# A hybrid recurrent/FFN trunk on one core: the order of loads at the front, one ring for late weights, and turned outputs inside y

## The chip, the core and the metric

The kernel runs on one core of a Trainium2 chip, in one launch. The time is the device time of one execution in microseconds, as the median of repeated runs. One execution more was taken with a profile; it has a time of its own, and all durations of single instructions come from it.

## What is computed

The reference is two residual layers over 2048 latent tokens of width 1024 with a prefix of 256 context tokens. Layer 0 is a bidirectional gated linear recurrence (HGRN2, 8 heads of 128, chunks of 64) and a gated FFN with convolution; layer 1, another mixer, is absent here (DEPTH is 1). Cut to what matters:

```python
D_MODEL, SEQ, CTX_LEN, HEADS, D_FF, CHUNK = 1024, 2048, 256, 8, 2816, 64
# adaLN: shift, scale and gate rows come from SiLU(c) @ w_ada (context: SiLU(c_ctx))
h = modulate(rmsnorm(x, g), shift, scale)          # latent and context
q, zf_fwd, zf_bwd, v, g = split(h @ w_in, 5)       # q = silu(q)
f = lb + (1 - lb) * sigmoid(zf);  k = 1 - f        # per direction
# S_t = diag(f_t) S_{t-1} + k_t v_t^T,  o_t = S_t^T q_t, both directions,
# each direction starting from its final context state
o = o_fwd + o_bwd
y = (rmsnorm(o per head) * silu(g)) @ w_out
x = x + gate1 * y
x = x + gate2 * convffn(modulate(rmsnorm(x), shift2, scale2))
```

The output is the latent stream, 2048 x 1024, in float32.

## The kernel before

Tokens are worked in 16 tiles of 128 (index t; the context is t = -2, -1). Every product is made of three matmuls: `split` (L76) writes an operand as a rounded high part, by ScalarE (L77), and the rest, by VectorE (L78); high x high, high x low and low x high are summed in PSUM. So each weight and each activation passes ScalarE and then VectorE before TensorE (PE) can use it. Five engines run their own instructions in order; the order on each engine is fixed at compile time, after the program's order and priorities. DMAs are issued by SP (queue rows named SPq) or by ScalarE (ACTq), also in order: an instruction that waits holds back what stands behind it on its engine.

Front (L179 to L230). The first two of six rows of the modulation are `sil` times w_ada. 16 loads of 512 KB go into tiles `wada`, in turn by ScalarE and SP, interleaved with 64 matmuls (L202) into four PSUM rows `mps`; the sigmoid that makes `sil` stands ahead of the loads on ScalarE's queue. Three early token tiles are loaded between them (`early_x`: load, square with a sum at L97, root on VectorE and GpSimd at L73 and L74, scale at L100). Four copies `m` (L209), 16 transposes `mt` (L212) and small sums give scale A1 and shift B1 (L215 to L217). With these, `transpose_mod` (L104) turns a token tile into `hm` (PE at L109, ScalarE at L113 or VectorE at L116), and `put_tok` (L147) splits `hm` into the tokens `tok`. Tiles 1 to 4 are squared and scaled ahead of their turn.

`put_tok` keeps tiles 0 to 7 in SBUF. Tiles 8 to 15 go through one staging tile, tag `stg` (one buffer), whose content SP stores to DRAM. `normalize` needs a tile to hold the squares, which nobody reads (`junk`): for `load_x` it comes from the same tag `stg`.

Scan (`mixer_scan`, L264, to about 1283 us). Two halves g of the tokens, and in each 8 heads. For each head five weight blocks are loaded (`load_w`, L166: `raw` of pool `rawp` with two buffers, SP at L168) and split; `acc` (L322) runs 8 x 3 matmuls per block of 512 tokens (L327 to L329), and after each k a `tick` runs what an agenda holds for that time. The results feed ScalarE copies (vt L465, kt L459, v L472, q and g L367), VectorE scans (S L380) and small matmuls (tr L471 and L457, kv L530, o L555). Heads 2 to 5 of the first half make the tokens 8 to 15 (`make_tok`, L338) in pairs.

In the second half `ada_rest` (L582) makes the other four modulation rows. Here 32 loads of w_ada go by SP (L589) through `raw`, and VectorE accumulates (L591, L593); each row is then stored. `out_weight` (L613) prepares the output projection's weight: parts 0 to 3 through `raw`, parts 4 to 7 in `wraw`, a tile that takes the context tokens' place (tag `cxt`) when they are no longer needed; these four are split behind the scan. `keep_gate` (L572) stores each head's gates to DRAM, by SP (L577).

Output stage (`mixer_out`, about 1283 to 1560 us). The tiles go from 15 down to 0. For each, `load_stash` (L876) brings `kq` and `og` from DRAM into two buffers each. `heads` (L881) multiplies by the backward state (oi, L895), adds into og (L899), squares (L902), updates the state (L904), sums (L907) and scales og by the root (VectorE L912, ScalarE L914). `heads_T` (L917) turns og (tp, L924), multiplies by the gate (L926) and splits into `ghl`. `residual(n)` (L930) is y: 24 matmuls for each of two halves n (L935 to L937), added to the latent (L938). The loop turns tile t-1 at the start of the iteration of t, ahead of `heads(t-2)`. norm2 and the stores of the FFN's operands lie beside it. The FFN follows and runs to the end.

Of the kernel before, what the change touches and what calls it, by code (L numbers as in the profile page):

```python
# [11 lines left out]
F32 = mybir.dt.float32  # L12
# [33 lines left out]
def body(ctx, tc, a, out):  # L46
# [125 lines left out]

    def load_x(xt, t):
        x_tile(xt, t)
        junk = xp.tile([128, D], F32, name="junk", tag="stg", bufs=1)
        normalize(xt, junk, gp, on_act=True)
# [4 lines left out]
    with ExitStack() as c0:  # L181
        p0s = pool_(c0, "p0s", space=PSUM)
        act.activation(sil, vec[:, V_C:V_C + 16], AF.Sigmoid)
        dve.tensor_tensor(sil, sil, vec[:, V_C:V_C + 16], OP.mult)
        silv = sil.rearrange("p (two k) -> p k two", two=2)
# [3 lines left out]
        def early_x(t):  # L189
# [3 lines left out]
            load_x(staged[t], t)  # L193

        for k in range(KT):
            for i in range(2):
                n = 2 * k + i
                wt = ada[n // 4][:, n % 4]
                (sp if i else act).dma_start(
                    wt, a["w_ada"][k * 128:(k + 1) * 128, i * D:(i + 1) * D])  # L200
                for n in range(2):
                    pe.matmul(mps[2 * i + n], silv[:, k, :], wt[:, n * 512:(n + 1) * 512],  # L202
                              start=k == 0, stop=k == KT - 1)
            if 3 <= k < 6:
                early_x(k - 5)
        head0 = {ty: load_w(0, ty) for ty in HEAD0[:2]}
# [7 lines left out]
        for i in (1, 0):  # L214
            dve.tensor_tensor(B1[i], mt[:, 0:8, i], vec[:, V_BA:V_BA + 8], OP.add)  # L215
            dve.tensor_tensor(A1[i], mt[:, 8:16, i], vec[:, V_BA + 8:V_BA + 16], OP.add)
            dve.scalar_tensor_tensor(A1[i], A1[i], 1.0, vec[:, V_NG:V_NG + 8], OP.add, OP.mult)  # L217
        hms = [xp.tile([128, KT, 128], F32, name="hm", tag="hm", bufs=1),
               xp.tile([128, KT, 128], F32, name="hm", tag="xt", bufs=1),
# [7 lines left out]
        with tc.issue_after(ada_done.ins):  # L227
            head0.update({ty: load_w(0, ty) for ty in HEAD0[2:]})
        for t in range(1, 5):
            early_x(t)  # L230

# [32 lines left out]
    def mixer_scan():  # L264
# [73 lines left out]
        def make_tok(t, xt=None):  # L338

            got = [xt]  # L340
            hms = []

            def load():
                got[0] = xp.tile([128, D], F32, name="xt", tag="xt", bufs=1)
                load_x(got[0], t)

            def put(g):
                if g == 0:
                    hms.append(xp.tile([128, KT, 128], F32, name="hm", tag="hm", bufs=1))
                transpose_mod(got[0], hms[0], g, ps, A1[0], B1[0], "tr", 1, g)  # L350
                put_tok(hms[0], t, g)

            puts = [lambda: put(0), lambda: put(1)]
            return puts if xt is not None else [load] + puts
# [217 lines left out]
        def keep_gate(h, t0, g):  # L572
            for i in range(UT):
                if is_late(h, t0 + i):
                    pool.tensor_copy(late[:, 1], g[:, i])
                else:
                    sp.dma_start(stash[t0 + i][:, 1, h, 1], g[:, i])  # L577

# [3 lines left out]
        def ada_rest():  # L582

            for i in range(4):
                acc_ = xp.tile([128, D], F32, name="acc", tag="xt", bufs=1)
                c = (2 + i) * D
                for k in range(KT):
                    raw = rawp.tile([128, D], F32, name="raw", tag="raw")
                    sp.dma_start(raw, a["w_ada"][k * 128:(k + 1) * 128, c:c + D])  # L589
                    if k == 0:  # L590
                        dve.tensor_scalar(acc_, raw, sil[:, k:k + 1], None, OP.mult)  # L591
                    else:
                        dve.scalar_tensor_tensor(acc_, raw, sil[:, k:k + 1], acc_, OP.mult, OP.add)  # L593
                    if k < KT - 1:
                        yield
                row = rawp.tile([1, D], F32, name="row", tag="raw")
                for n in range(2):
# [12 lines left out]

        wraw = []

        def out_weight(k):  # L613

            if k < 4:
                raw = rawp.tile([128, D], F32, name="raw", tag="raw")
            else:
                if not wraw:
                    wraw.append(hq.tile([128, 4, D], F32, name="wraw", tag="cxt", bufs=1))
                raw = wraw[0][:, k - 4]  # L620
            sp.dma_start(raw, a["w_out"][k * 128:(k + 1) * 128, :])
# [100 lines left out]
        for k in range(4, KT):  # L722
            split(w_out_part("h", k), w_out_part("l", k), wraw[0][:, k - 4])

# [139 lines left out]
    def mixer_out(c3):  # L864
# [64 lines left out]

        def residual(n, lat, gh, gl):  # L930

            cs = slice(n * 512, (n + 1) * 512)
            y = ps.tile([128, 512], F32, name="y", tag="y")
            for k in range(KT):
                pe.matmul(y, gh[:, k], w_out_part("h", k)[:, cs], start=k == 0, stop=False)  # L935
                pe.matmul(y, gh[:, k], w_out_part("l", k)[:, cs], start=False, stop=False)
                pe.matmul(y, gl[:, k], w_out_part("h", k)[:, cs], start=False, stop=k == KT - 1)  # L937
            dve.tensor_tensor(lat[:, cs], lat[:, cs], y, OP.add)  # L938

# [62 lines left out]
        def load_lat(t):  # L1002
            lat = wn.tile([128, D], F32, name="lat", tag="lat")
            sp.dma_start(lat, a["x"][t * 128:(t + 1) * 128])
            return lat

        next_lat = load_lat(NT - 1)
        for t in range(NT - 1, -1, -1):
            lat = next_lat
            steps = ()  # L1010
            if prev is not None:
                xn = wn.tile([128, D], F32, name="xn", tag="xn", bufs=1)
                steps = norm_steps(prev, xn)
            if t and t < NT - 1:
                gs.append(heads_T(t - 1, ogs.pop(0)))
            if t > 1:
# [6 lines left out]
            g = gs.pop(0)  # L1023
            residual(0, lat, *g)
            if t == NT - 1:
                gs.append(heads_T(t - 1, ogs.pop(0)))
            if t > 2:
# [519 lines left out]
```

## Time and profile before

| | us |
|---|---|
| median of 3 runs | 2827.68 |
| lowest, highest | 2827.45, 2831.03 |
| profiled execution, its own time | 2832.5 |
| its span | 2830.8 |
| mean granted TensorE clock | 0.986 |

Times in a profile are microseconds from the start of the span, and the profiled execution has 1.7 us around it. A row of the timeline gives start, duration, engine, line, operation, output and input with their shape, a count, and in brackets how long the engine had been idle and who released it. A row of waits gives the engine and its line, what it waited for, the total, how often, and the longest. PE is TensorE, PEld its weight load, DVE VectorE, ACT ScalarE, POOL GpSimd, SP SyncE.

### The profile page before, as it was taken

The page shows a single profiled execution, that of the slowest core. Times are in us where ns is not written, and L with a number is a line of the kernel's source. Part 1 is how long each engine was busy: PE and PEld are TensorE (multiplying, and loading weights), DVE is VectorE, ACT ScalarE, POOL GpSimd, SP SyncE. Part 2 cuts the span into 40 slices and gives each one's busy share as a digit, 9 for nine tenths or more (in the row PEclk, how much of TensorE's full clock was granted, in tenths as well). Part 3 has the DMA queues.
Part 4 walks back from the last instruction along what each step waited for, and adds up shares of the span by engine and source line. Part 5 has one row for each costly group of instructions (what it writes and reads, how often), then busy time and mean ns, then how long its engine had stood idle before and what let it go on. Part 6 is the DMA issues. An engine that isn't in the chain of part 4 may idle for free.

```text
span 2830.8 us, 41935 instructions
## 1 busy us (share of the span) xinstructions
PE 2742.5 (97%) x16072; PEld 2274.9 (80%) x16072; DVE 1981.7 (70%) x2804; ACT 1151.0 (41%) x1910; POOL 560.1 (20%) x882
## 2 busy tenths in 40 slices
PE   7999999999999999998999899999999999999998
PEld 3788888888888788886888688888888888877887
DVE  3655556656666667657887788877877777576887
ACT  5424343433232223334656444444444444333343
POOL 2111101111111111111110443333344331000001
PEclk8999999999999999998999999999999999999999
DMA  5122232213533424216777422226322223987663
GB/s 224 49 69 88 87 112 90 89 59 126 202 89 94 129 81 127 90 54 237 278 294 293 186 90 90 84 69 231 141 86 90 90 86 105 321 286 251 194 200 123
DMA packets 223777, 402.18 MB, mean 142 GB/s; under 512 B 29012, under 2 KB 136404, under 8 KB 217816
## 3 DMA queue, kind: packets, MB, share of 16 engines
q1 hardware_dynamic: 220552, 391.24, 41.5%
q10 hardware_dynamic: 3024, 8.26, 0.8%
q8 instruction: 126, 2.06, 0.3%
q14 instruction: 75, 0.61, 0.1%
HBM read 289.04 MB, written 110.38 MB: 141 GB/s over the span
## 4 chain that ended last, share of the span: by engine, by line
PE 74%; DMA 11%; DVE 9%; issue 2%; ACT 2%; POOL 1%; SPq 1%; DVEq 0%; POOLq 0%; ACTq 0%
PE z L327 9%; PE z L329 9%; PE z L328 9%; PE zd L777 3%; PE zd L779 3%; PE zd L780 3%; PE zc L777 3%; PE zc L780 3%; PE zc L779 3%; PE za L777 3%; PE za L780 3%; PE za L779 3%; DMA lr<-m 2%; PE kv L530 2%; PE y L1377 2%
## 5 line engine op out<-in xcount | busy, mean ns | idle before, releaser
L327 PE MATMUL z<-tok,w 128*128 128x512 f32 x1280 | 517.6, 405 | 0.0
L329 PE MATMUL z<-tok,w 128*128 128x512 f32 x1280 | 503.7, 394 | 0.5 <-DVE w L78 0.5
L328 PE MATMUL z<-tok,w 128*128 128x512 f32 x1280 | 503.6, 393 | 0.0
L78 DVE TENSOR_TENSOR w<-raw,w 128x512 fp32r<-128x512 f32 (+1 forms) x260 | 239.5, 925 | 142.1 <-ACT w L77 139.8
L329 PEld LDWEIGHTS z<-tok,w 128*128 128x128 f32 x1280 | 242.0, 189 | 52.3 <-DVE w L78 1.0
L327 PEld LDWEIGHTS z<-tok,w 128*128 128x128 f32 x1280 | 242.8, 190 | 48.4 <-issue 3.6
L328 PEld LDWEIGHTS z<-tok,w 128*128 128x128 f32 x1280 | 242.7, 190 | 44.8 <-issue 0.2
L77 ACT ACTIVATE w<-raw 128x512 fp32r<-128x512 f32 (+1 forms) x260 | 195.9, 760 | 186.6 <-PE zd L780 77.3
L1377 PE MATMUL y<-wd,mh 128*128 128x512 f32 x600 | 234.4, 391 | 3.6 <-ACT X L1412 3.3
L1379 PE MATMUL y<-wd,ml 128*128 128x512 f32 x600 | 234.5, 391 | 1.2 <-DVE ml L78 1.2
L1378 PE MATMUL y<-wd,mh 128*128 128x512 f32 x600 | 234.0, 390 | 0.0
L78 DVE TENSOR_TENSOR w<-s,w 128x512 fp32r<-128x512 f32 x126 | 121.4, 968 | 53.8 <-ACT w L77 53.0
L380 DVE TENSOR_TENSOR_SCAN S<-F,d 128x528 f32<-128x528 f32 (+1 forms) x80 | 91.6, 1145 | 91.2 <-ACT F L363 90.6
L777 PE MATMUL zc<-rT,w 128*128 128x512 f32 x352 | 137.1, 389 | 1.2 <-DVE uv L1264 1.0
L779 PE MATMUL zc<-rT,w 128*128 128x512 f32 x352 | 136.9, 389 | 0.0
L780 PE MATMUL zc<-rT,w 128*128 128x512 f32 x352 | 136.9, 389 | 0.0
L1377 PEld LDWEIGHTS y<-wd,mh 128*128 128x128 f32 x600 | 113.0, 188 | 28.1 <-ACT X L1412 4.1
L77 ACT ACTIVATE w<-s 128x512 fp32r<-128x512 f32 x126 | 78.2, 627 | 138.5 <-POOL s L833 81.9
L1379 PEld LDWEIGHTS y<-wd,ml 128*128 128x128 f32 x600 | 112.9, 188 | 26.5 <-DVE ml L78 3.0
L1378 PEld LDWEIGHTS y<-wd,mh 128*128 128x128 f32 x600 | 113.0, 188 | 23.5
L777 PE MATMUL za<-rB,w 128*128 128x512 f32 x336 | 130.7, 389 | 0.0
L779 PE MATMUL za<-rB,w 128*128 128x512 f32 x336 | 130.7, 389 | 0.0
(323 smaller groups left out, 6223.3 us busy)
## 6 DMA issues: line engine op xcount, KB each, us to landing
raw<-in_w_up_dram SPq DMA_DIRECT2D x88, 512.0 KB, 3.9
raw<-in_w_in_dram SPq DMA_DIRECT2D x80, 512.0 KB, 3.9
lr<-m SPq DMA_DIRECT2D x49, 512.0 KB, 5.7
m<-r SPq DMA_DIRECT2D x66, 256.0 KB, 4.4
raw<-in_w_ada_dram SPq DMA_DIRECT2D x32, 512.0 KB, 3.9
kq<-stash SPq DMA_DIRECT2D x15, 1024.0 KB, 6.4
og<-stash SPq DMA_DIRECT2D x15, 1024.0 KB, 5.4
u<-in_w_down_dram SPq DMA_DIRECT2D x51, 256.0 KB, 3.8
```

The source lines that it names most:

```text
L77: act.activation(h, src, AF.Copy)
L78: dve.tensor_tensor(l, src, h.bitcast(F32), OP.subtract)
L327: pe.matmul(z, w[:, 0, k], h, start=k == 0, stop=False, skip_group_check=True)
L328: pe.matmul(z, w[:, 0, k], l, start=False, stop=False, skip_group_check=True)
L329: pe.matmul(z, w[:, 1, k], h, start=False, stop=k == KT - 1, skip_group_check=True)
L380: dve.tensor_tensor_scan(flat(S[:, d]), flat(F[:, d]), flat(d1[:, 0:ns]), 0.0, OP.mult, OP.max)
L777: pe.matmul(o, w[:, 0, k], r[:, :, 0, k], start=start and k == 0, stop=False, skip_group_check=True)
L779: pe.matmul(o, w[:, 0, k], r[:, :, 1, k], start=False, stop=False, skip_group_check=True)
L780: pe.matmul(o, w[:, 1, k], r[:, :, 0, k], start=False, stop=k == 3, skip_group_check=True)
L1377: pe.matmul(z, lh, rh, start=start, stop=False, skip_group_check=True)
L1378: pe.matmul(z, lh, rl, start=False, stop=False, skip_group_check=True)
L1379: pe.matmul(z, ll, rh, start=False, stop=stop, skip_group_check=True)
```

## The change

Front: all 16 loads of w_ada are issued first, eight by ScalarE and eight by SP, and the sigmoid comes behind them; the three early tiles follow. Squares of tiles 1 to 4 are issued behind the four copies `m`. Squares: a tile made by `make_tok` puts its squares into the `hm` tile that it will fill anyway, no longer into `stg`. Ring: w_ada's later rows, the stored rows and parts 4 to 7 of the output weight take turns in a ring of four tiles in the context's place; `raw` keeps w_in and the parts 0 to 3. Gates: the last head's gates of tiles 8 to 15 are stored by ScalarE. Output stage: `heads_T(t-1)` is called in the middle of the first half of y, after 12 of its 24 matmuls, instead of at the start of the iteration.

```diff
--- before.py
+++ after.py
@@ -170,9 +170,13 @@
         split(w[:, 0], w[:, 1], raw.rearrange("p (k n) -> p k n", k=KT))
         return w
 
-    def load_x(xt, t):
+    def new_hm():
+        return xp.tile([128, KT, 128], F32, name="hm", tag="hm", bufs=1)
+
+    def load_x(xt, t, hm=None):
         x_tile(xt, t)
-        junk = xp.tile([128, D], F32, name="junk", tag="stg", bufs=1)
+        junk = hm.rearrange("p k n -> p (k n)") if hm is not None else \
+            xp.tile([128, D], F32, name="junk", tag="stg", bufs=1)
         normalize(xt, junk, gp, on_act=True)
 
 
@@ -180,8 +184,6 @@
     staged = {}
     with ExitStack() as c0:
         p0s = pool_(c0, "p0s", space=PSUM)
-        act.activation(sil, vec[:, V_C:V_C + 16], AF.Sigmoid)
-        dve.tensor_tensor(sil, sil, vec[:, V_C:V_C + 16], OP.mult)
         silv = sil.rearrange("p (two k) -> p k two", two=2)
         mps = [p0s.tile([2, 512], F32, name=f"mps{n}") for n in range(4)]
         ada = [place(i, [128, 4, D], F32, "wada") for i in range(4)]
@@ -192,17 +194,20 @@
             staged[t] = gp.tile([128, D], F32, name="x0", tag=tag, bufs=1 if tag == "kd" else 2)
             load_x(staged[t], t)
 
+        wts = [ada[n // 4][:, n % 4] for n in range(2 * KT)]
+        for n, wt in enumerate(wts):
+            (sp if n % 2 else act).dma_start(
+                wt, a["w_ada"][n // 2 * 128:(n // 2 + 1) * 128, n % 2 * D:(n % 2 + 1) * D])
+        act.activation(sil, vec[:, V_C:V_C + 16], AF.Sigmoid)
+        dve.tensor_tensor(sil, sil, vec[:, V_C:V_C + 16], OP.mult)
+        for t in range(-2, 1):
+            early_x(t)
         for k in range(KT):
             for i in range(2):
-                n = 2 * k + i
-                wt = ada[n // 4][:, n % 4]
-                (sp if i else act).dma_start(
-                    wt, a["w_ada"][k * 128:(k + 1) * 128, i * D:(i + 1) * D])
                 for n in range(2):
-                    pe.matmul(mps[2 * i + n], silv[:, k, :], wt[:, n * 512:(n + 1) * 512],
+                    pe.matmul(mps[2 * i + n], silv[:, k, :],
+                              wts[2 * k + i][:, n * 512:(n + 1) * 512],
                               start=k == 0, stop=k == KT - 1)
-            if 3 <= k < 6:
-                early_x(k - 5)
         head0 = {ty: load_w(0, ty) for ty in HEAD0[:2]}
         m2 = [gp.tile([2, 512], F32, name="m2", tag="qg"[n // 2], bufs=2) for n in range(4)]
         for n in range(4):
@@ -215,7 +220,7 @@
             dve.tensor_tensor(B1[i], mt[:, 0:8, i], vec[:, V_BA:V_BA + 8], OP.add)
             dve.tensor_tensor(A1[i], mt[:, 8:16, i], vec[:, V_BA + 8:V_BA + 16], OP.add)
             dve.scalar_tensor_tensor(A1[i], A1[i], 1.0, vec[:, V_NG:V_NG + 8], OP.add, OP.mult)
-        hms = [xp.tile([128, KT, 128], F32, name="hm", tag="hm", bufs=1),
+        hms = [new_hm(),
                xp.tile([128, KT, 128], F32, name="hm", tag="xt", bufs=1),
                gp.tile([128, KT, 128], F32, name="hm", tag="S", bufs=1)]
         for g in range(2):
@@ -226,8 +231,8 @@
                 put_tok(hm, t, g)
         with tc.issue_after(ada_done.ins):
             head0.update({ty: load_w(0, ty) for ty in HEAD0[2:]})
-        for t in range(1, 5):
-            early_x(t)
+            for t in range(1, 5):
+                early_x(t)
 
 
         l0, l1 = vec[:, V_LB:V_LB + 16], vec[:, V_LB + 16:V_LB + 32]
@@ -342,11 +347,12 @@
 
             def load():
                 got[0] = xp.tile([128, D], F32, name="xt", tag="xt", bufs=1)
-                load_x(got[0], t)
+                hms.append(new_hm())
+                load_x(got[0], t, hms[0])
 
             def put(g):
-                if g == 0:
-                    hms.append(xp.tile([128, KT, 128], F32, name="hm", tag="hm", bufs=1))
+                if not hms:
+                    hms.append(new_hm())
                 transpose_mod(got[0], hms[0], g, ps, A1[0], B1[0], "tr", 1, g)
                 put_tok(hms[0], t, g)
 
@@ -574,7 +580,16 @@
                 if is_late(h, t0 + i):
                     pool.tensor_copy(late[:, 1], g[:, i])
                 else:
-                    sp.dma_start(stash[t0 + i][:, 1, h, 1], g[:, i])
+                    (act if h == NH - 1 and t0 >= HT else sp).dma_start(
+                        stash[t0 + i][:, 1, h, 1], g[:, i])
+
+        spare = []
+
+        def spare_raw():
+            if not spare:
+                spare.extend([hq.tile([128, 4, D], F32, name="spare", tag="cxt", bufs=1), 0])
+            spare[1] += 1
+            return spare[0][:, (spare[1] - 1) % 4]
 
         ones = small("ones", (128, 1))
         pool.memset(ones, 1.0)
@@ -585,7 +600,7 @@
                 acc_ = xp.tile([128, D], F32, name="acc", tag="xt", bufs=1)
                 c = (2 + i) * D
                 for k in range(KT):
-                    raw = rawp.tile([128, D], F32, name="raw", tag="raw")
+                    raw = spare_raw()
                     sp.dma_start(raw, a["w_ada"][k * 128:(k + 1) * 128, c:c + D])
                     if k == 0:
                         dve.tensor_scalar(acc_, raw, sil[:, k:k + 1], None, OP.mult)
@@ -593,7 +608,7 @@
                         dve.scalar_tensor_tensor(acc_, raw, sil[:, k:k + 1], acc_, OP.mult, OP.add)
                     if k < KT - 1:
                         yield
-                row = rawp.tile([1, D], F32, name="row", tag="raw")
+                row = spare_raw()[0:1]
                 for n in range(2):
                     z = ps.tile([1, 512], F32, name="z", tag="pj", bufs=3)
                     pe.matmul(z, ones, acc_[:, n * 512:(n + 1) * 512], start=True, stop=True)
@@ -608,16 +623,14 @@
             gate_row(g1, 0, 2 * D)
             g1s.append(g1)
 
-        wraw = []
+        wraw = {}
 
         def out_weight(k):
 
             if k < 4:
                 raw = rawp.tile([128, D], F32, name="raw", tag="raw")
             else:
-                if not wraw:
-                    wraw.append(hq.tile([128, 4, D], F32, name="wraw", tag="cxt", bufs=1))
-                raw = wraw[0][:, k - 4]
+                raw = wraw[k] = spare_raw()
             sp.dma_start(raw, a["w_out"][k * 128:(k + 1) * 128, :])
             dve.scalar_tensor_tensor(raw, raw, vec[:, V_GN:V_GN + 1], g1s[0], OP.mult, OP.mult)
             if k < 4:
@@ -720,7 +733,7 @@
                 head(g, h)
         run(1 << 30)
         for k in range(4, KT):
-            split(w_out_part("h", k), w_out_part("l", k), wraw[0][:, k - 4])
+            split(w_out_part("h", k), w_out_part("l", k), wraw[k])
 
     mixer_scan()
     c1.close()
@@ -927,7 +940,7 @@
                 split(gh[:, hs], gl[:, hs], g)
             return gh, gl
 
-        def residual(n, lat, gh, gl):
+        def residual(n, lat, gh, gl, between=None):
 
             cs = slice(n * 512, (n + 1) * 512)
             y = ps.tile([128, 512], F32, name="y", tag="y")
@@ -935,6 +948,8 @@
                 pe.matmul(y, gh[:, k], w_out_part("h", k)[:, cs], start=k == 0, stop=False)
                 pe.matmul(y, gh[:, k], w_out_part("l", k)[:, cs], start=False, stop=False)
                 pe.matmul(y, gl[:, k], w_out_part("h", k)[:, cs], start=False, stop=k == KT - 1)
+                if k == KT // 2 - 1 and between:
+                    between()
             dve.tensor_tensor(lat[:, cs], lat[:, cs], y, OP.add)
 
         def norm_steps(lat, xn):
@@ -1004,6 +1019,9 @@
             sp.dma_start(lat, a["x"][t * 128:(t + 1) * 128])
             return lat
 
+        def turn():
+            gs.append(heads_T(t - 1, ogs.pop(0)))
+
         next_lat = load_lat(NT - 1)
         for t in range(NT - 1, -1, -1):
             lat = next_lat
@@ -1011,8 +1029,6 @@
             if prev is not None:
                 xn = wn.tile([128, D], F32, name="xn", tag="xn", bufs=1)
                 steps = norm_steps(prev, xn)
-            if t and t < NT - 1:
-                gs.append(heads_T(t - 1, ogs.pop(0)))
             if t > 1:
                 ogs.append(heads(t - 2, steps))
             else:
@@ -1021,9 +1037,9 @@
             if t:
                 next_lat = load_lat(t - 1)
             g = gs.pop(0)
-            residual(0, lat, *g)
+            residual(0, lat, *g, between=turn if 0 < t < NT - 1 else None)
             if t == NT - 1:
-                gs.append(heads_T(t - 1, ogs.pop(0)))
+                turn()
             if t > 2:
                 gts[t - 3] = load_stash(1, t - 3)
             if t == 1:
```

## The prediction

> **What bounds the kernel now.** I read the page first: how full TensorE is.
>
> ```profile
> span 2830.8 us, 41935 instructions
> PE 2742.5 (97%) x16072; PEld 2274.9 (80%) x16072; DVE 1981.7 (70%) x2804; ACT 1151.0 (41%) x1910; POOL 560.1 (20%) x882
> ```
>
> TensorE stands idle for 2830.8 - 2742.5 = 88.3 us of the span. The change removes no matmul, so it can win only from these 88.3 us and from time at a reduced clock. The waits of PE, grouped, say which stalls they are (engine and line, releaser: total us, times, longest).
>
> ```profile
> PE tr L471 <- ACT vt L465: 13.0, 5, 3.1
> PE mt L212 <- ACT m L209: 9.5, 1, 9.5
> PE oi L895 <- DMA kq<-stash: 9.3, 1, 9.3
> PE tp L924 <- ACT og L914: 6.0, 5, 1.3
> PE tp L924 <- DVE og L912: 1.6, 2, 1.2
> PE tp L924 <- PE y L937: 0.9, 1, 0.9
> ```
>
> These are 40.3 of the 88.3 us, and each belongs to one part of the change: values waiting for their copy in the scan (13.0), modulation rows at the front (9.5), the first load of the output stage (9.3), and the turning of the gated outputs (6.0 + 1.6 + 0.9 = 8.5). So I cost the change stall by stall. A cost counts only where it reaches PE.
>
> **A. Front.** The rows are the timeline's (start, duration, engine, line), then the loads' own row (duration of an issue: least, median, most) and two windows (PE, PEld, DVE, ACT and POOL busy; granted clock, DMA share, GB/s).
>
> ```profile
> 1.73 1.28 ACT L183 ACT_TABLE_LOAD   x1 [1.73 <-PEq L1538]
> 4.40 5.12 ACTq L199 DMA_DIRECT2D wada<-in_w_ada_dram  x4
> 5.00 28.92 PE L202 MATMUL mps<-wada,sil 128*2 128x512 f32 x64 [5.00 <-DVE sil L184]
> 39.55 1.06 ACT L97 ACTIVATE junk<-x 128x1024 f32<-128x1024 f32 x1 [1.48 <-DMA x<-in_x_dram]
> 44.66 1.05 ACT L209 ACTIVATE m<-mps 2x512 f32<-2x512 f32 x2
> 47.52 0.17 DVE L215 TENSOR_TENSOR B<-mt,vec 128x8 f32<-128x8 f32 x1 [2.51 <-PE mt L212]
> L199 ACTq DMA_DIRECT2D wada<-in_w_ada_dram x8: 334/353/460, 0.8 to 20.2; - x8
> 8.00:12.00 4.00, 4.00 (x11) 0.85 (x10) 1.07 (x4) 0.00 (x0) 4.00 (x8) 1.00 1.02 419
> 40.00:44.00 4.00, 0.62 (x6) 0.65 (x7) 0.15 (x1) 3.08 (x6) 0.55 (x1) 0.50 0.01 2
> ```
>
> Before, PE multiplies from 5.00 to 33.92; then the copies of the four m rows stand in ACT's order behind squares such as that at 39.55, and the shift B is ready at 47.52. After, the copies come before those squares. But now the sigmoid, on which every mps matmul waits, stands behind eight load issues on ACT. Issues are not free: the four from 4.40 held the queue 5.12 us where one takes 0.35, so a later issue waits for an earlier load to land. By the compiled program the last of ACT's eight waits for the seventh load of all. A 512 KB load takes 0.524 MB / 419 GB/s = 1.25 us; if the first lands just before 5.0, the seventh lands near 5.0 + 6 x 1.25 = 12.5. With the issue (0.35), the table load (1.28) and sigmoid and product (0.4), PE starts near 14.6 and ends at 14.6 + 28.9 = 43.5, 9.6 us later than before. The 9.5 us wait falls to about 1; four copies at 0.53 and the turning then bring B at about 46 instead of 47.5. PE no longer idles into the 0.50 clock of the second window, worth some 1 to 2 us more. Against that, the squares and scalings of four tiles (about 2.4 us each, 9.6 us of ACT) now stand behind 46, in front of the tokens that they feed. I take -1, with -4 (all of the 1.5 and the clock) and +5 (half of the squares on the path) as ends. Moving SP's loads ahead of its x loads costs nothing more: DMA stands at 1.02 of its engines, and the order alone changes.
>
> **B. The square's junk tile.** The rows: ACT's timeline, PE's windows behind the stall, ACT's waits, and ACT at the other tile of a pair.
>
> ```profile
> 291.24 1.06 ACT L97 ACTIVATE junk<-xt 128x1024 f32<-128x1024 f32 x1 [6.28 <-DMA tok<-stg]
> 294.00:296.00 2.00, 2.00 (x7) 1.53 (x6) 0.00 (x0) 0.86 (x2) 0.00 (x0) 0.59 0.00 0
> 296.00:298.00 2.00, 2.00 (x11) 1.89 (x10) 0.00 (x0) 0.00 (x0) 0.00 (x0) 0.56 0.00 0
> ACT junk L97 <- DMA tok<-stg: 18.7, 3, 6.3
> 250.59 0.60 ACT L459 ACTIVATE kt<-tr 128x512 f32<-128x512 f32 x1 [1.09 <-PE tr L457]
> ```
>
> Three times ACT stands about 6.2 us (18.7 in all) because the square writes its unused output into the tile that still waits for the store of tokens; the copy of vt (L465) is behind it. These are three of the five vt waits: 13.0 less the two of the later stage (4.9, below) gives 8.1 us. Each is followed by 4 us at a clock of 0.59 and 0.56, which loses 4 x (1 - 0.575) = 1.7 us. Junk in the hm tile needs no store to finish, only the split of the tile before, so all three go: 8.1 + 3 x 1.7 = 13.2 us at most. The Trainium skill (TensorE: Matmul & The Clock Gate, Part 1) says that the clock halves after an idle window of about 3.4 us; by that these gaps of 2.7 us would cost no clock and B would be worth 8.1 alone. The two windows say otherwise, and the trace decides. Cost: at the other tile of four pairs the square, now early, stands ahead of the copy at 250.59 and can hold it by part of a square, 0.7 us each, up to 2.8. I take -13.2 + 2.2 = -11, with -13 and -6 as ends (clock loss not regained).
>
> **C. Rows of w_ada, 720 to 1190 us.** ACT's waits, one of them in its place, and PE's waits from 700 to 1000.
>
> ```profile
> ACT w L77 <- DMA raw<-in_w_in_dram: 53.9, 19, 7.2
> 979.49 1.06 ACT L77 ACTIVATE w<-raw 128x1024 fp32r<-128x1024 f32 x1 [7.21 <-DMA raw<-in_w_in_dram]
> PE tr L471 <- ACT vt L465: 4.9, 2, 3.1
> PE tr L457 <- ACT kt L459: 1.6, 1, 1.6
> PE kv L530 <- ACT v L472: 1.3, 1, 1.3
> PE o L555 <- DVE states L533: 1.0, 1, 1.0
> PE z L329 <- DVE w L78: 0.5, 1, 0.5
> ```
>
> Before, w_in loads (next head) alternate with w_ada loads in two raw buffers, so a weight is late by up to 7.21 us, and ACT, in order, holds vt, kt and v behind it. PE loses 4.9 + 1.6 + 1.3 + 1.0 + 0.5 = 9.3 us, and about 1.5 of clock by the price in B for its one long gap. With the ring in the context's place w_in keeps both raw buffers, as in the half before 720, where no PE wait on a weight's load shows. But the compiled order now bunches w_ada: runs of four to ten loads on SP, each waiting for DVE to free a slot, with stores and w_in loads behind them, and up to three accumulations in a row on DVE ahead of a scan. Three are about 3 x 1.28 = 3.8 us, where before they stood singly. I take -6: the 10.8, less one new stall of the size of 979.49's (3.1 and 1.6 of clock, together 4.7). Ends: -11 and +8 (four such stalls).
>
> **D. Turning inside y.** PE and ACT at one tile, SP's reload of og, its use by DVE, the two ends of one y matmul, and the load's landing (page, last column).
>
> ```profile
> 1396.22 1.06 PE L924 MATMUL tp<-ident,og 128*128 128x128 f32 x8 [1.27 <-ACT og L914]
> 1395.43 1.28 ACT L914 ACTIVATE og<-og,rs 128x128 f32<-128x128 f32 x4 [5.87 <-POOL rs L74]
> 1418.69 0.32 SPq L876 DMA_DIRECT2D og<-stash  x1
> 1428.44 1.48 DVE L899 TENSOR_TENSOR og<-og,oi 128x512 f32<-128x512 f32 x2
> 1385.30 0.39 PE L937 MATMUL y<-wo,ghl 128*128 128x512 f32 x1
> 1385.53 0.39 PE L935 MATMUL y<-wo,ghl 128*128 128x512 f32 x1
> og<-stash SPq DMA_DIRECT2D x15, 1024.0 KB, 5.4
> ```
>
> PE reaches tp about 1.3 us before L914 gives its first output, tile after tile. Turned after 12 matmuls of y it comes 12 x 0.23 = 2.8 us later, behind oi too, so the wait of 1.3 is covered with over a microsecond to spare: up to -8.5 us for the loop. The cost lies on SP: og's buffer comes free that much later, some 4.5 us with oi. In the shorter case above og is issued at 1418.69, lands at 1424.1 and is read at 1428.44: 4.3 us to spare, all but used up. What then is late is L899, whose chain to L914 has itself gained about 3 us, so little should reach PE. I take -6, ends -8.5 and +3.
>
> **E, F. The stage's two ends.** First load and first use; then the first w_up weight.
>
> ```profile
> 1287.12 0.38 SPq L876 DMA_DIRECT2D kq<-stash  x1
> 1290.61 0.32 SPq L876 DMA_DIRECT2D og<-stash  x1
> 1295.53 0.69 DVE L899 TENSOR_TENSOR og<-og,oi 128x512 f32<-128x512 f32 x1 [0.43 <-DMA og<-stash]
> 1536.92 0.63 ACT L77 ACTIVATE w<-raw 128x512 fp32r<-128x512 f32 x1 [1.65 <-DMA raw<-in_w_up_dram]
> ```
>
> With the last gates stored by ACT, SP is spared their issues and reaches kq about 2 us earlier (five at 0.4). But the first y hangs on og, issued at 1290.61 behind DVE's last splits of the output weight, and those splits are behind ACT's copies, now behind seven store issues at some 0.4 us. E: -1, ends -4 and +3. The Trainium skill (DMA: Bandwidth & Descriptors, Issuing engines are not separate DMA queues) says that another issuing engine saves only the time of the issue; that is E's whole gain here. F: the first w_up loads take og's place, released about 3 us later, and ACT waits 1.65 on one already: +1, ends -1 and +4. What follows (the FFN) has the same program.
>
> **The sum.** -1 - 11 - 6 - 6 - 1 + 1 = -24 us. The profiled execution took 2832.5 us (2830.8 and 1.7 around it) and becomes 2808.5; it was 4.8 us above the median of the timed runs, 2827.7, which becomes 2803.7. I forecast 2804 us.
>
> **Rivals.** *Half the gain.* The copies and junk do what they should, but C gives nothing (bunches replace the late weights) and the front pays its late squares: -24 + 6 + 6 = -12, some 2816. For it: PE starts its first matmul 9.6 us later, and C's SP runs. Chance 0.23. *More gain*: every part near its good end except the front, -4 - 13 - 10 - 8 - 2 = -37, 2791; for it, no engine but PE is over 70% busy; against, each gain uncovers the next wait. Chance 0.1. *Slower, by the bunches.* SP is in order: if each run of w_ada loads blocks it until DVE has freed slots, the w_in loads behind it are late at every run, and PE stalls as at 979.49, 4.7 us a time. There are some nine runs. The other five parts give -18, so the sign turns when C reaches +18, or (18 + 10.8) / 4.7, six stalls; with all nine, C is 42 - 10.8 = +31 and the time 2827.7 + 13 = 2841. Against it: DVE is 70% busy, and in the compiled order the accumulations of a run stand ahead of the next weights' splits. Chance 0.1. *Not what it says*: the parts move stalls without removing them, B included (hm is still being split when the square comes): within 5 us of 2827.7. Against: hm's split ends long before 291. Chance 0.05.
>
> **How the numbers follow.** The forecast has 0.52, with 2804 and its own 2797 to 2811. The range 2790 to 2821 takes in half the gain and most of the larger one, and leaves out the slower rival, the idle one and small tails, under 2 in 10. About 0.2% (5.7 us) can be told from no change. Faster: 0.52 + 0.23 + 0.1 = 0.85; same 0.05; slower 0.10.
>
> **What would show it.** Right: no vt wait near 291, 375 and 459 and no low clock behind; B1 at about 46 with mps from 14 to 44; no wait of ACT on w_in loads above 3 us after 720; no tp wait on og. Wrong: PE waits on w or F near SP's w_ada runs, oi waiting for kq or og in the output stage, the first tokens well after 75.

## The result and the profile after

| | before | after |
|---|---|---|
| median of 12 runs, us | 2826.24 | 2836.40 |
| lowest to highest | 2820.88 to 2831.03 | 2830.76 to 2841.79 |
| profiled execution, span | 2832.5, 2830.8 | 2833.5, 2831.8 |
| ratio, 95% interval | | 1.0038, 1.0029 to 1.0048 |

The change makes the kernel slower by 10 us; 24 less were forecast. The two profiled executions differ by 1.0 us only: that of before is longer than any of its 12 timed runs, 6.3 above their median, and that of after is 2.9 below its own. So the traces are compared by stages, and the times by the ratios.

The page of the kernel after, its first lines:

```profile
span 2831.8 us, 41982 instructions
PE 2735.7 (97%) x16072; PEld 2267.8 (80%) x16072; DVE 1978.9 (70%) x2804; ACT 1149.9 (41%) x1910; POOL 563.6 (20%) x882
```

PE is idle for 96.1 us as against 88.3. The waits of PE after:

```profile
PE mps L208 <- DVE sil L202: 15.2, 1, 15.2
PE y L948 <- DVE lat L953: 13.4, 7, 4.6
PE oi L908 <- DMA kq<-stash: 9.8, 1, 9.8
PE tp L109 <- DVE xn L962: 8.5, 7, 2.1
PE tp L109 <- ACT xt L100: 5.8, 3, 2.3
```

The vt waits (13.0), the mt wait (9.5) and the tp waits on og (8.5) are gone. In their place PE waits for the sigmoid, for scaled tiles (xt), and in the output stage for the latent and the norm. Where time was lost and won follows from the starts of like matmuls, counted one by one over PE's timeline from 0 (us, after less before; +2.2 at z 80 means that this z matmul starts 2.2 us later in the changed kernel):

| matmul | after - before | the stretch up to it | us |
|---|---|---|---|
| z 80 | +2.2 | front, tiles 1 to 4 | +2.2 |
| z 730 | +10.4 | tiles 5 to 7 among them | +8.2 |
| z 1680 | +1.7 | the four pairs of tiles 8 to 15 | -8.7 |
| z 2400 | +1.8 | rest of the first half | +0.1 |
| z 3800 | -11.6 | second half, w_ada rows | -13.4 |
| y 48 | -13.3 | end of the scan, first tile out | -1.7 |
| y 624 | -0.4 | output stage, tiles 14 to 3 | +12.8 |
| y 720 | +7.4 | its last tiles | +7.8 |
| first zc | +4.1 | start of the FFN | -3.4 |
| end | +1.0 | FFN, the same program | -3.1 |

Two places lose 29 us together, the tokens of tiles 5 to 7 (8.2) and the output stage (12.8 and 7.8).

**Tiles 5 to 7.** ACT's timeline after: the scalings of tiles 1 to 3, then the squares of tiles 5, 6 and 7. Behind them PE's turnings of tiles 5 and 6:

```profile
58.82 3.21 ACT L100 ACTIVATE x<-x,rs 128x1024 f32<-128x1024 f32 x3
86.94 1.05 ACT L97 ACTIVATE hm<-xt 128x1024 f32<-128x1024 f32 x1
99.38 1.06 ACT L97 ACTIVATE hm<-xt 128x1024 f32<-128x1024 f32 x1 [0.27 <-DVE tok L78]
113.12 1.06 ACT L97 ACTIVATE hm<-xt 128x1024 f32<-128x1024 f32 x1 [1.40 <-DMA xt<-in_x_dram]
92.07 0.66 PE L109 MATMUL tp<-ident,xt 128*128 128x128 f32 x4 [2.27 <-ACT xt L100]
104.01 0.86 PE L109 MATMUL tp<-ident,xt 128*128 128x128 f32 x4 [1.86 <-ACT xt L100]
```

The timeline of before, the first of these squares:

```profile
61.16 1.06 ACT L97 ACTIVATE junk<-xt 128x1024 f32<-128x1024 f32 x1 [2.32 <-DMA xt<-in_x_dram]
```

Tile 5 was squared at 61.16 and now at 86.94: its junk goes into the only hm, and hm is in use for tiles 1 to 4 until they are split (VectorE's last split of tile 4 ends at 86.4). The square of tile 6 waits for tile 5 to leave hm ("DVE tok L78"), 12.4 us behind; that of tile 7 comes 13.7 us later still, and there the profile names the load of its x. From tile 8 on the gain is 8.7 of the 11 forecast, and PE's windows behind the former stall at 290 stand at full clock:

```profile
294.00:296.00 2.00, 2.00 (x10) 1.67 (x9) 2.00 (x4) 1.32 (x2) 0.00 (x0) 1.00 0.01 2
296.00:298.00 2.00, 2.00 (x10) 1.65 (x10) 2.00 (x3) 1.15 (x2) 0.00 (x0) 1.00 0.87 164
```

**Output stage.** The timeline after, at two tiles: PE's turning, VectorE's gate products (L939) and adds (L912), SP's reload, what PE waits for; then VectorE's waits on og from 1310 to 1515.

```profile
1395.57 1.03 PE L937 MATMUL tp<-ident,og 128*128 128x128 f32 x8
1400.85 0.69 DVE L939 TENSOR_TENSOR og<-tp,og 128x512 f32<-128x512 f32 x1
1403.32 0.69 DVE L939 TENSOR_TENSOR og<-tp,og 128x512 f32<-128x512 f32 x1
1407.85 0.32 SPq L889 DMA_DIRECT2D og<-stash  x1
1413.83 0.69 DVE L912 TENSOR_TENSOR og<-og,oi 128x512 f32<-128x512 f32 x1 [2.93 <-DMA og<-stash]
1420.99 1.06 PE L109 MATMUL tp<-ident,xn 128*128 128x128 f32 x8 [1.73 <-DVE xn L962]
1425.41 0.47 PE L948 MATMUL y<-wo,ghl 128*128 128x512 f32 x1 [1.57 <-DVE lat L953]
DVE og L912 <- DMA og<-stash: 22.5, 9, 3.6
```

Before, both products of a tile followed its turning at once, and VectorE hardly waited for og (timeline of before and the same waits; PE's row of 1396.22 stands in the prediction):

```profile
1396.90 1.28 DVE L926 TENSOR_TENSOR og<-tp,og 128x512 f32<-128x512 f32 x2
DVE og L899 <- DMA og<-stash: 1.1, 1, 1.1
```

After, the second product ends at 1404.0, 7.4 us behind the end of the turning at 1396.6. The reload of og (1407.85) waits for the split behind it and lands late; VectorE, in order, stands 2.93 us at L912; the norm and the latent's add behind it are late, and PE waits for both.

### The profile page after: what moved, and what is told of

It reads as the page before. It is cut to its first block, busy times and chain, and to the rows that moved or that the text cites. A ratio compares the mean times of both kernels' runs of the same rounds, so it can differ in the third digit from the quotient of the medians.

```text
span 2831.8 us, 41982 instructions
## 1 busy us (share of the span) xinstructions
PE 2735.7 (97%) x16072; PEld 2267.8 (80%) x16072; DVE 1978.9 (70%) x2804; ACT 1149.9 (41%) x1910; POOL 563.6 (20%) x882
## 4 chain that ended last, share of the span: by engine, by line
PE 67%; DMA 7%; DVE 6%; issue 1%; ACT 1%; POOL 1%; SPq 0%; DVEq 0%; ACTq 0%; POOLq 0%
PE z L332 8%; PE z L334 8%; PE z L333 7%; PE y L1395 3%; PE y L1393 3%; PE y L1394 3%; PE zc L790 3%; PE zd L790 3%; PE zd L793 3%; PE zc L793 3%; PE zd L792 3%; PE zc L792 3%; PE za L793 3%; PE za L790 3%; PE za L792 3%; PE kv L536 1%
## 5 line engine op out<-in xcount | busy, mean ns | idle before, releaser
L78 DVE TENSOR_TENSOR w<-raw,w 128x512 fp32r<-128x512 f32 (+1 forms) x260 | 239.4, 925 | 144.6 <-ACT w L77 140.7
L78 DVE TENSOR_TENSOR w<-s,w 128x512 fp32r<-128x512 f32 x126 | 121.3, 967 | 52.5 <-ACT w L77 51.7
```

Source lines behind the costliest of these rows:

```text
L78: dve.tensor_tensor(l, src, h.bitcast(F32), OP.subtract)
```

## The experiments

Kernels that were run together share their runs of the kernel before, and each ratio is to these. The medians of those shared runs lie between 2822.0 and 2825.3, beside 2826.2 in the result, so a difference of two medians is given by the ratios too where this matters.

**Which losses are apart.** junk_late: tiles 5 to 7 square into stg again.

```diff
-                hms.append(new_hm())
-                load_x(got[0], t, hms[0])
+                if t < HT:
+                    load_x(got[0], t)
+                else:
+                    hms.append(new_hm())
+                    load_x(got[0], t, hms[0])
```

> The changed kernel, but tiles 5 to 7 square into the stg tile again; tiles 8 to 15 still square into hm. Theory J (the square of one tile waits until the tile before has left hm, so the tokens of tiles 5 to 7 come one behind another): the 60th to 240th z matmul regain 8 to 9 us of the 10.8 us that the changed kernel lags at z 720, and the time falls from 2836 to about 2828. Rival F (the sigmoid behind eight loads and the late squares of tiles 1 to 4 make the lag): z 720 still lags by 9 to 11 us, time 2836.

Measured: 2827.03, ratio 1.0007 (0.9998 to 1.0017), 9.4 us less than the changed kernel (9 by the ratios). At z 730 the lag is +3.2 instead of +10.4 (the 10.8 of the expectation): 7.2 us come back, a little less than J's 8 to 9. J holds, and F is left with the 3.2.

gate_tile: the product in a tile of its own.

```diff
-                g = og[:, hs, 1]
-                dve.tensor_tensor(g, tp, g, OP.mult)
+                g = wk.tile([128, 4, 128], F32, name="gm", tag="gm", bufs=1)
+                dve.tensor_tensor(g, tp, og[:, hs, 1], OP.mult)
```

> The changed kernel, but the turned outputs times the gate go into a small tile of their own, so that the place of og is free for its reload when the gate has been read and not only when the product has been split. Theory O (the loss in the output stage is VectorE standing in its order at L912 for the late og, with the norm and the latent's add behind it): VectorE's 22.5 us of waits on og fall below 5, PE's waits on lat and xn (21.9 us) below 6, the first to last oi take 211 to 214 us as against 222.0, time about 2819 to 2825. Rival Y (turning in the middle of y costs by itself, since the gate product and its split now stand ahead of the latent's add): waits on lat stay above 8 us, time 2834 to 2837.

Measured: 2827.95, ratio 1.0012 (1.0003 to 1.0021). VectorE's waits on og from 1310 to 1515:

```profile
DVE og L912 <- DMA og<-stash: 8.1, 7, 2.7
```

Waits on og fall to 8.1, not below 5, and the time by 8.5 us (7 by the ratios), where O asked for 11 to 17. PE's waits on lat are gone, against Y, and those on xn come to 6.0; but PE now waits 9.2 us for the ScalarE half of the split (ghl). Neither theory fits: the late og counts, but something else makes it late or costs beside it.

turn_back: the heads turned at the start of the iteration.

```diff
+            if t and t < NT - 1:
+                turn()
             if t > 1:
                 ogs.append(heads(t - 2, steps))
...
-            residual(0, lat, *g, between=turn if 0 < t < NT - 1 else None)
+            residual(0, lat, *g)
```

> The changed kernel, but heads are turned at the start of the iteration as before. Theories O and Y alike: the output stage is as long as before (oi 211.7 us from first to last, the 720th y no later than the 624th asks), 18 to 22 us come back, time 2815 to 2818. If the output stage suffers from its start instead (gates stored by ScalarE, a late og), the time stays above 2828.

Measured: 2820.41, ratio 0.9986 (0.9977 to 0.9994): 16 us less than the changed kernel (15 by the ratios), short of the 18 asked. From y 48 to y 767 the trace follows that of before within 0.3 us, so the whole loss of the output stage (20.7 in the traces) goes with the place of the call.

both: the edits of junk_late and turn_back.

> The changed kernel with tiles 5 to 7 squared into stg and the heads turned at the start of the iteration. If the two losses are apart from each other they add: 8 to 9 and 18 to 22 us less, time 2806 to 2810. By rival F the front's loss stays, 2815 to 2818.

Measured: 2810.23, ratio 0.9945 (0.9932 to 0.9958), 26.2 us less than the changed kernel (26 by the ratios); 9.4 and 16.0 add to 25.4 (8.8 and 14.7 to 23.5 by the ratios). The losses are apart. PE still waits for the turning here, 7.9 us in the stage, as before the change.

**The place of the turning, and the front.** pos0 and pos6 start from junk_late; pos0 calls `turn()` ahead of `residual(0)`, pos6 after k = 1 of y.

> The kernel of run junk_late (2827.0), but heads are turned between the 16 oi matmuls and the first y matmul, not after 12 of y. Theory O (what costs is how late og's place comes free; a reload that was 4.3 us early at the shortest loses 1.9 us of that here, against 4.6 us after 12 matmuls): VectorE waits under 6 us on og, no tp wait on og of the 7.9 us that run both still has, time 2803 to 2808. Rival Y (the gate product and split queued ahead of the latent's add on VectorE cost, wherever the turning stands behind oi): time 2818 to 2827.

> As pos0, but turned after 6 of y's matmuls. Theory O: the loss grows with the distance, between pos0 and junk_late, 2810 to 2820, with VectorE's waits on og between theirs. Rival Y: as long as junk_late, 2825 to 2829.

Measured: pos0 2816.18, ratio 0.9973 (0.9962 to 0.9983), pos6 2823.95, ratio 0.9996 (0.9987 to 1.0004), beside 2810.23 at the start of the iteration and 2827.03 after 12. VectorE's waits on og in pos0 and in pos6, from 1290 to 1515 (pos0's trace is of an execution of 2810.60, 5.6 below its median):

```profile
DVE og L915 <- DMA og<-stash: 14.9, 11, 3.3
```

```profile
DVE og L915 <- DMA og<-stash: 27.2, 13, 4.4
```

Both times lie between the ranges of O and Y. The loss grows with the distance, but it is there already in pos0, where only the 16 oi matmuls (1.95 us) come in front of the turning; O had asked for a gain there. So how much later the turning stands does not explain the loss by itself.

front_back (from both): the front as before the change. sig_first (from both) puts the sigmoid ahead of the loads again:

```diff
+        act.activation(sil, vec[:, V_C:V_C + 16], AF.Sigmoid)
+        dve.tensor_tensor(sil, sil, vec[:, V_C:V_C + 16], OP.mult)
         wts = [ada[n // 4][:, n % 4] for n in range(2 * KT)]
...
-        act.activation(sil, vec[:, V_C:V_C + 16], AF.Sigmoid)
-        dve.tensor_tensor(sil, sil, vec[:, V_C:V_C + 16], OP.mult)
```

> The kernel of run both (2810.2), but with the front as it was before the change (loads in turn with the matmuls, sigmoid first, squares of tiles 1 to 4 not held behind the copies). Run both lags 3.1 us at z 80; both theories (late squares S, late sigmoid P) take this lag away, time 2806 to 2808. If the lag is no more than the change of the clock's phase, 2810.

> The kernel of run both, but the sigmoid and its product stand ahead of the loads again; the loads all come first, and the squares stay behind the copies. Theory P (the sigmoid behind eight loads starts TensorE 10 us late): first mps at 5.0 as against 15.1, the lag at z 80 goes from +3.1 to -2 or less, time 2803 to 2807. Theory S (the four squares behind the copies are on the path of the tokens, and the copies end no earlier because the last load lands when it did): the lag at z 80 stays at +2 to +3, time 2809 to 2811.

Measured: front_back 2804.79, ratio 0.9926 (0.9913 to 0.9939), sig_first 2804.34, ratio 0.9923 (0.991 to 0.9936). PE after the change, and in sig_first:

```profile
15.21 29.49 PE L208 MATMUL mps<-wada,sil 128*2 128x512 f32 x64 [15.21 <-DVE sil L202]
```

```profile
4.89 30.16 PE L208 MATMUL mps<-wada,sil 128*2 128x512 f32 x64 [4.89 <-DMA wada<-in_w_ada_dram]
45.15 0.38 PE L332 MATMUL z<-cxt,w 128*128 128x256 f32 x1 [0.90 <-ACT cxt L77]
```

The first z comes at 45.15, against 51.62 in both and 52.09 before, and at z 80 the lag of +3.2 becomes -3.4. P holds: the late sigmoid took away what the early copies give. (In the compiled order of sig_first, as of the kernel before, two of ScalarE's eight issues still stand ahead of the sigmoid, at 0.80; the other six stand behind it.) Whether the whole new order beats the old one with the sigmoid first is not told by the times, which agree; the traces have sig_first 2.9 us ahead at z 240.

**What remains of D, and the other parts**, all from sig_first: pos0_gate (turned as in pos0, product as in gate_tile), start_gate (that tile alone), sp_gates (`sp.dma_start` for all gates), ring_back (rows of w_ada through `raw` again).

> The kernel of run sig_first (2804.3), but heads are turned between oi and y (as in run pos0, which was 6 us slower than run both) and the gate product goes into a tile of its own (as in run gate_tile), so that og's place is free some 4 us sooner. Theory O (the late reload of og is the whole cost): VectorE's waits on og fall from pos0's 14.9 to under 4 us, and the tp wait on og (7.9 us at the start of the iteration) is gone, time 2797 to 2802. Rival Y (the order on VectorE and ScalarE costs by itself): waits on xn and lat stay, time 2808 to 2812.

> The kernel of run sig_first with the gate product in a tile of its own and the heads turned at the start of the iteration: what that tile costs alone. Theory O: VectorE hardly waits on og here (1.0 us), so nothing is won, 2803 to 2806. Rival (the single tile makes the second product wait for the split of the first): 2806 to 2812.

> The kernel of run sig_first with the last gates stored by SP again. If the stores by ScalarE win SP two us for kq and nothing hangs on it, because og sets the first y: the first oi up to 2 us later, the first y and the time the same, 2803 to 2806. If kq is what counts: first y 2 us later, 2806.

> The kernel of run sig_first, but the late rows of w_ada and the stored rows go through raw again, in turn with w_in; the last parts of the output weight stay in the ring's tile. If the 13 us that all kernels with the ring gain between z 2400 and z 3800 are the ring's: they are lost, time 2815 to 2818, and ScalarE waits up to 7 us for w_in again. Rival (the gain comes from another phase of the loads): 2804 to 2810.

Measured: pos0_gate 2809.94, ratio 0.9946 (0.9934 to 0.9958); start_gate 2799.28, 0.9917 (0.9904 to 0.993); sp_gates 2800.84, 0.9916 (0.9902 to 0.9929); ring_back 2816.47, 0.9969 (0.9957 to 0.9981). pos0_gate's waits from 1255 to 1500:

```profile
PE tp L940 <- DVE gm L942: 6.8, 4, 2.0
DVE og L915 <- DMA og<-stash: 12.5, 8, 2.3
```

PE now waits for places of tp that VectorE's product frees late, so the product itself comes late. This fails O as it stood and points to VectorE's order; the time is in Y's range, but the waits on xn and lat that Y asked for are not there (1.3 and 0). sp_gates and start_gate come out 2 to 4 us below the ranges that were asked (from 2803), but cannot be told from sig_first, as the intervals overlap. In ring_back the gain of z 2400 to z 3800 is gone (-16.1 and -16.0 to before, -15.4 and -28.8 in sig_first), and ACT, which waits 3.8 us for w_in in all of sig_first, waits again:

```profile
ACT w L77 <- DMA raw<-in_w_in_dram: 54.7, 18, 7.3
```

**The rank of the products.** Each engine's order is made from the program's order and priorities, and an instruction's place in it is called its rank here. The change moves `heads_T(t-1)` behind `heads(t-2)` in the program, and so on every engine. From the timelines of PE, VectorE and SP, the medians over the 14 tiles whose turning moved (12 that have a reload), in us behind the end of the turning:

| kernel | second product ends | og's reload issued |
|---|---|---|
| before | 1.3 | 6.4 |
| after | 9.8 | 12.4 |
| pos0 | 8.9 | 12.9 |
| both, sig_first | 1.3, 1.3 | 6.4, 6.4 |

In after and in pos0 the tiles take turns: the product ends some 7.5 us behind in one (5.6 in pos0) and some 13 in the next (15 in pos0). So in pos0 the product and the reload are about as far behind the turning as in after, though the turning itself is earlier.

So the three runs that follow leave the turning late and give the product and the split the rank of the iteration's start: after_prio on the changed kernel, prio12 on sig_first turned after 12, prio0 on sig_first turned between oi and y. `begin` keeps the priority at the start of the iteration, and `heads_T` gets it as `ahead`.

```diff
                 g = og[:, hs, 1]
-                dve.tensor_tensor(g, tp, g, OP.mult)
-                split(gh[:, hs], gl[:, hs], g)
+                with tc.high_priority(offset=tc.cur_priority - ahead if ahead else 0):
+                    dve.tensor_tensor(g, tp, g, OP.mult)
+                    split(gh[:, hs], gl[:, hs], g)
...
-            gs.append(heads_T(t - 1, ogs.pop(0)))
-
+            gs.append(heads_T(t - 1, ogs.pop(0), begin[0]))
...
+            begin[0] = tc.cur_priority
```

> The changed kernel, turned after 12 matmuls of y as it is, but with the gate products and their splits given the rank of the iteration's start in the order of VectorE and ScalarE. Theory R (the rank of the products makes og late): second product within 3 us of the last tp as against 10.3, VectorE's waits on og under 6 us as against 22.5, time as run turn_back or up to 8 us less: 2812 to 2822. Rival Y (turning inside y costs in itself, by og's place freed 4.6 us later): 2828 to 2837.

> The kernel of run sig_first (2804.3), turned after 12 matmuls of y, with the products ranked as in after_prio. Theory R: no tp wait on og (7.9 us in sig_first's stage) and no new wait above 4 us in sum, 2797 to 2804. Rival Y: 2815 to 2821, as far above sig_first as junk_late is above both.

> As prio12, but turned between oi and y, which frees og 2.8 us sooner. Theory R: 2796 to 2803, at most as long as prio12. Rival Y: 2808 to 2812, as far above sig_first as pos0 is above both.

Measured: after_prio 2814.76, ratio 0.9973 (0.9962 to 0.9983); prio12 2799.28, 0.9917 (0.9903 to 0.993); prio0 2797.19, 0.9911 (0.9898 to 0.9925). The timeline of after_prio, and VectorE's waits from 1290 to 1515:

```profile
1401.20 1.03 PE L937 MATMUL tp<-ident,og 128*128 128x128 f32 x8
1404.60 1.28 DVE L940 TENSOR_TENSOR og<-tp,og 128x512 f32<-128x512 f32 x2
1407.81 0.32 SPq L889 DMA_DIRECT2D og<-stash  x1
DVE og L912 <- DMA og<-stash: 3.3, 3, 2.1
```

R holds, and Y's 2828 to 2837 is ruled out: the new rank takes 21.6 us from the changed kernel (18 by the ratios, as the kernel before was faster in these runs too), no less than undoing the turning does; in the traces the stretch from y 48 to y 720 is 22.4 us shorter than in the changed kernel. The product is not quite as near as was asked (median 3.6 us, not 3), but og is reissued 5.7 us behind the turning, and the waits on it are nearly gone. The run moves the product and both halves of the split together, so which of them counts most is not shown. prio12 and prio0 have no wait on lat left and almost none on og; PE in prio0, from 1290 to 1515:

```profile
PE tp L940 <- issue: 1.5, 1, 1.5
PE tp L109 <- DVE rs L73: 1.2, 2, 1.0
PE tp L940 <- DVE og L928: 1.0, 1, 1.0
```

In the traces the stage from y 48 to y 720 is 2.5 us (prio12) and 3.4 us (prio0) shorter than before. By the ratios prio0 is 3 us under sig_first (7 by the medians), with intervals that overlap, so the times do not tell them apart. prio0 is faster than both kernels of the case.

## Why the prediction was wrong, step by step

- **A (-1, found +2.2).** B was forecast for 46 and came at 46.60, the start of mps for 14.6 and came at 15.21; these sizes held, and +2.2 lies within the part's ends (-4 and +5). What was off is the balance: the copies gain little because the sigmoid is late. With the sigmoid first, the same step wins 3.4 us at z 80.

```profile
46.60 0.17 DVE L220 TENSOR_TENSOR B<-mt,vec 128x8 f32<-128x8 f32 x1 [10.25 <-PE mt L217]
```

Eight issues held ACT for 12.6 us, since later ones wait for earlier loads: the sixth to the eighth came at 7.94, 10.52 and 13.07, and the second to the fourth of ACT's loads had landed at 7.92, 10.49 and 13.05. The Trainium skill (DMA: Bandwidth & Descriptors, Issuing engines are not separate DMA queues) calls the time of an issue usually small beside the transfer; here the "small" did not hold, as these 12.6 us show:

```profile
0.81 12.60 ACTq L199 DMA_DIRECT2D wada<-in_w_ada_dram  x8
14.73 0.22 ACT L201 ACTIVATE sil<-vec 128x16 f32<-128x16 f32 x1
```

- **B (-11, found -8.7 and +8.2).** The stalls and the low clock went as worked out. What failed is a cost put at nothing. The sentence "Junk in the hm tile needs no store to finish, only the split of the tile before" holds, but was priced for the pairs of tiles 8 to 15 alone. Tiles 5 to 7 come by the same `make_tok`, one close behind the other; for them the split of the tile before was the later event, as junk_late shows.
- **C (-6, found -13.4).** The mechanism is right, by ring_back, and the term was mis-sized, beyond its better end of -11: the new stall that was taken off did not come, and the 10.8 of waits and clock turned into 13.4. The slower rival, the bunches of w_ada loads, did not happen: PE is busy for 100.00 of 100 us in every hundred from 700 to 1200, as in this window of after, where before had 96.32:

```profile
900.00:1000.00 100.00, 100.00 (x786) 83.76 (x785) 61.91 (x88) 30.68 (x52) 13.45 (x24) 1.00 0.39 120
```

- **D (-6, found +20.7).** This is the step that turned the sign. It failed at "The cost lies on SP". The turning was followed on PE and on SP, but the gate products that come with it were not followed on VectorE, though a moved step counts on every queue. They fell behind the next tile's adds and sums, and the ScalarE half of the second split (1406.45 in the stretch shown) behind the next tile's scaling by the root; og's place came free not 4.5 us later by distance alone, but 6 us more by rank (12.4 instead of 6.4 behind the turning). Then "so little should reach PE" failed too: VectorE waits for og in order, with the norm and the latent's add behind it, in a stage in which it is busy for 86.5 of 100 us before the change (1400 to 1500).
- **E (-1, found -1.7).** Within its ends. sp_gates shows that the stores' engine makes no difference that can be told.
- **F (+1, found -3.4).** Outside its ends (-1 and +4), to the good side. The same gain stands in junk_late and gate_tile (-3.5 and -3.3), whose output stage is long too, and not in turn_back, both and after_prio (0.0, -0.2 and -0.5). So it goes with D's loss; why is not shown.
- The rivals: "half the gain" and "more gain" had the sign wrong, and the slower rival had the wrong place. "Not what it says" named the mechanism of tiles 5 to 7 (hm still being split when the square comes), but set it aside by the tiles near 291. The mechanism that decided most, a queue order on VectorE, was not among them.
- The signs: those named for "right" came true (no vt wait and no low clock at 290, 375 and 459, B at 46.60, no wait of ACT on w_in loads for a weight at all, no tp wait on og), and the kernel is slower all the same. They look at the waits that go, and not at those that come in their place.

The Trainium skill's window of 3.4 us (TensorE: Matmul & The Clock Gate, Part 1), which the prediction set against the rows, is not borne out here: PE's gap ahead of 293 us was 2.75 us before, and with it gone the windows 294:298 stand at 1.00 where they were at 0.59 and 0.56.

What stays open is whether the covered turning wait is worth anything in the time: prio0 and prio12 are not told apart from sig_first, as the intervals overlap.

## What to carry to other kernels

When a call is moved in a program that a scheduler orders, it changes rank on every engine: follow each of its instructions on each queue, and the release of each buffer that they hold, before pricing the engine that one wants to help. A scratch output put into a tile that will be filled anyway inherits that tile's whole life; look at every caller, the closest spaced ones first. Loads issued from a compute engine can hold that engine until earlier loads have landed, as the 12.6 us here, so what gates the next stage goes ahead of them.

## What was not expected

That eight load issues, each about 0.35 us by itself, would hold the sigmoid for some 12 us was forecast; that this would cost 6.6 us at z 80 (+3.2 in both, -3.4 in sig_first), more than the early copies give, was not. And a rank alone, with not one instruction more or less (41982 in both traces), was worth 21.6 us by the medians (2836.40 to 2814.76) and 18 by the ratios.
